# Layer 0's output product: a third pair of row tiles by Strassen's scheme

## The chip, the cores and the metric

The program runs on one core of one Trainium2 chip. The core has five instruction streams. PE is the matrix engine (TensorE), with its weight loads shown apart as PEld. DVE (VectorE) and ACT (ScalarE) do element-wise work, POOL is GpSimd, and SP issues most of the transfers, in the order of its own queue. The metric is the device time of one execution in microseconds (us); lower is better. Three runs of the kernel before lie between 919.55 and 919.75, with a median of 919.62.

## What is computed

Two layers of a mixer on 256 tokens of width 2048, in float32. Of each layer only the last step, the product with `w_out`, is touched:

```python
h = rmsnorm(x, norm_g[l])
proj = h @ w_in[l]                       # 256 x 2048 by 2048 x 7168
...
y = jnp.concatenate([y_a, y_d, y_m], axis=-1) @ w_out[l]   # 256 x 2048 by 2048 x 2048
x = x + y
```

`y_a` are the first 768 columns of `y` (six tiles of 128, from a gated convolution), `y_d` the next 768 (six heads of differential attention), and `y_m` the last 512 (four heads of attention to the memory tokens).

## The kernel before

**Products in three parts.** PE multiplies a 128 x 128 tile of the turned activations by 128 x 512 weights. To keep float32's precision, each operand is split into a rounded part `hi` (a copy on ACT) and the rest `lo` (a subtraction on DVE), and each product is three matmuls: hi·hi, hi·lo, lo·hi. `block` (line 309) walks over the 16 row tiles (128 of the 2048 rows) in chunks of two: `load_w` (L286) issues a 512 KB load into `raw` (four buffers) on SP, splits it on ACT and DVE into `hi` and `lo` (four chunks' worth of buffers), and 2 row tiles x 2 token tiles x 3 = 12 matmuls use it. So the loads may run up to four chunks ahead of the splits, and the splits up to four chunks ahead of the matmuls.

**Side work.** Everything else hangs on a counter of chunks. `run_side` (L231), called after each chunk, raises the counter by one and takes one step of each generator in `tasks` that is due; a generator's `yield n` makes it due n chunks later, and `later(g, n)` starts it n chunks from now. `settle` (L250) is called before a chunk uses a row tile of the activations: if the tile has not been made yet, it calls `run_side(now=True)`, which takes a step of every waiting generator at once, until it is made. Most instructions may be moved by a scheduler that works before the launch; those given to `keep_in_program_order` (`pin`) keep their order among themselves on their engine. On the chip each engine then takes its instructions strictly in the order so fixed.

**The output product of a layer** (from L1213 on). Column blocks 0 and 1 (512 columns each) are done in the plain way and end in `leave`: `finish` adds the accumulators to the residual `xs`, and in layer 0 `x_next` (L801) is put on the list for the next layer. `x_next` for a quarter q of the columns issues `xd<-xs` (residual to memory, 512 KB), two chunks later `xt<-xd` (four transfers back as strips), two later `turn_strips` (L784, a transpose on DVE), and then `split_T` (L257) for the four row tiles 4q to 4q+3 of the next layer's activations `xT`, two per chunk.

Column blocks 2 and 3, the last 1024 columns, are done together. `near` is the pair of accumulators for block 2 and `far` that for block 3. In layer 0 two pairs of row tiles, (6,7) and (8,9), are multiplied by Strassen's scheme in Winograd's form for all 1024 columns at once, by `seven` (L368): 7 products of 3 matmuls where the plain way has 8. `seven` loads the pair's weights as two `wide` tiles of 512 KB each into the buffers named in `homes`, and takes the sums of the token tiles from `sums`, made ahead by `all_sums` (L1203) and `token_sums` (L353). Four of the seven results are shared through the accumulators `x`; `collect` (L1256) adds them to the residual in three steps, and the second of these ends block 2 with `leave(2, near, n=3)`. The pairs stand at the chunk positions in `places` within the list `rest` of the remaining row tiles, 12 in layer 0. `rest` is walked once for `near` (with the pairs between) and once for `far`. In layer 1, the last, three pairs are taken.

**The next layer** opens with the column block 3 of `w_in`, on row tiles 0 to 11 (the first three quarters, six chunks), then block 0 on the same twelve, and only then the last quarter.

Names of buffers touched: `sums` n lies in tag `mkT0` for n = 0 and in `v` for n = 1; the pairs' `wide` tiles lie in `sh` (first) and in `bgx` and `ga` (second). `bgT` holds the turned gate of the convolution, `mqT` the turned queries and later the convolution's input, `mv` the values of the memory tokens. All three have been read for the last time in layer 0 when the convolution of the layer is done; in layer 1 `bgT`, `mqT` and `mv` are filled anew, `mv` by the generator `fetch` (L1026), 32 chunks after the layer's start.

Of the kernel before, what the change touches and what calls it, by code (L numbers as in the profile page):

```python
# [21 lines left out]
DEPTH = 2  # L22
# [8 lines left out]
MH = W_MEM // P  # L31
# [17 lines left out]
def encoder(ctx: ExitStack, tc: tile.TileContext, x, mem, norm_g, w_in, conv_w, conv_b,  # L49
# [4 lines left out]
    def pool(name, bufs, space=None):  # L54
        kw = {"space": space} if space is not None else {}
        return ctx.enter_context(tc.tile_pool(name=name, bufs=bufs, **kw))
# [4 lines left out]
    keep = pool("keep", 1)  # L61
    tmp = pool("tmp", 2)
# [8 lines left out]
    def nm(s):  # L71
        uid[0] += 1
        return f"{s}_{uid[0]}"
# [279 lines left out]
    def token_sums(stat, k, home):  # L353

        f = tmp.tile([P, 2, SEQ], F32, tag="nat", name=nm("f"), bufs=3)
        pin(nc.vector.tensor_tensor(f, stat[:, 0, k:k + 2, :].bitcast(F32), stat[:, 1, k:k + 2, :].bitcast(F32), ALU.add))
        a11, a21, a12, a22 = f[:, 0, 0:P], f[:, 0, P:SEQ], f[:, 1, 0:P], f[:, 1, P:SEQ]
        s = tmp.tile([P, 4, P], F32, tag="nat", name=nm("sums"), bufs=3)
        yield 1
        pin(nc.vector.tensor_tensor(s[:, 0], a21, a22, ALU.add))  # L360
        pin(nc.vector.tensor_tensor(s[:, 2], a11, a21, ALU.subtract))
        pin(nc.vector.tensor_tensor(s[:, 1], s[:, 0], a11, ALU.subtract))
        pin(nc.vector.tensor_tensor(s[:, 3], a12, s[:, 1], ALU.subtract))
        yield 1
        pin(nc.scalar.copy(home[:, 0], s))
        pin(nc.vector.tensor_tensor(home[:, 1], s, home[:, 0].bitcast(F32), ALU.subtract))
# [331 lines left out]
    spare, yTs, gates, summed_heads = {}, {}, {}, set()  # L698
# [251 lines left out]
    mkT, mv, stm, away = [], [], [], []  # L950
# [86 lines left out]
    while s < DEPTH * KT:  # L1037
        l, k = divmod(s, KT)
# [24 lines left out]
    for l in range(DEPTH):  # L1063
# [18 lines left out]
        for b in order:  # L1082
# [4 lines left out]
            if b == 3:  # L1087
                v = keep.tile([P, NT, W_DIFF], F32, tag="v", name=nm("v"))
                ga = keep.tile([P, NT, W_DIFF], F32, tag="ga", name=nm("ga"))
# [20 lines left out]
        mqT = keep.tile([P, MH, SEQ], F32, tag="mqT", name=nm("mqT"))  # L1110
# [22 lines left out]
        bgT = None  # L1133
# [67 lines left out]
        sums = []  # L1201

        def all_sums(l, yT, sums):  # L1203
            for n, tag in enumerate(("mkT0", "v") if l + 1 < DEPTH else ("mkT0", "mkT1", "v")):
                while tag == "v" and (l, MH // 2 - 1) not in summed_heads:
                    yield 1
                sums.append(keep.tile([P, 2, 4, P], F32R, tag=tag, name=nm("sums")))
                yield from token_sums(yT, CG + 2 * n, sums[n])
                yield 1

        tasks.append(later(all_sums(l, yT, sums), 1))
        acc = x_block([(C_X + NB, 256), (C_C + NB, 256)])
        scaled(both_rows(ux, 4, 6), [a[:, 0:256] for a in acc], R2)  # L1213
# [9 lines left out]
        final = l + 1 == DEPTH  # L1223
# [22 lines left out]
            if b == 0:  # L1246
                leave(b, accs[b])

        places = (2, 6, 8) if final else (2, 6)
        paired = [CG + 2 * n for n in range(len(places))]  # L1250
        homes = [((tmp, tag),) * 2 for tag in ("sh", "e", "sh")] if final else [((tmp, "sh"),) * 2, ((keep, "bgx"), (keep, "ga"))]
        rest = [k for k in heads + convs if not CG <= k < CG + 2 * len(places)]
        near, far = accumulators(), accumulators()
        x = [pl.tile([P, NB], F32, tag=tag, name=nm("x")) for pl, tag in ((ps_s, "s"), (ps_s, "s"), (ps_t, "t"), (ps_t, "t"))]
# [71 lines left out]
```

## Time and profile before

| | |
|---|---|
| median of three runs | 919.62 us |
| profiled execution | 919.16 us, of which the span of the instructions is 917.4 us |
| busy in the span: PE, PEld, DVE, ACT, POOL | 911.9, 757.3, 720.1, 515.8, 38.3 us |
| granted PE clock | 1.0 throughout |
| moved by transfers | 215.15 MB, 235 GB/s in the mean |
| layer 0's last 1024 columns on PE | about 464 to 507 us of the span |

The profile lists for each engine the busy time of its instructions, and its queries list groups of instructions, instructions in order of time, waits, and the busy time of every engine in a stretch of time. A matmul's listed duration covers its whole way through the array; the next one starts well before it ends, so the rate of PE is read from starts, not from durations. `acc<-hi,yT` reads: written by the program's tile `acc`, from `hi` and `yT`. Times in timelines count from the start of the span.

### The profile page before, as it was taken

Reading aid. Unit: us, or ns where it says so; the run is one execution under the profiler, and the core shown is the slowest. Engines: PE = TensorE matmul, PEld = TensorE weight load, DVE = VectorE, ACT = ScalarE, POOL = GpSimd, SP = SyncE. Lnnn points to the kernel's source line nnn. Section 1 sums busy time; section 2 is a strip of 40 time slices with the busy share of each in tenths; the row PEclk is TensorE's granted clock in tenths of the full one; section 3 lists DMA queues with packets and bytes.
Section 4 is the critical chain, followed back from the end, with each engine's and each line's share of the span. In section 5 each row is a group of like instructions: output and inputs, shape, how many; then the busy total and the mean of one; then the engine's idle time right before and its main releaser. Section 6 shows DMA issues by size and latency. Waiting matters only on the chain.

```text
span 917.4 us, 12407 instructions
## 1 busy us (share of the span) xinstructions
PE 911.9 (99%) x4161; PEld 757.3 (83%) x4161; DVE 720.1 (78%) x1293; ACT 515.8 (56%) x798; POOL 38.3 (4%) x68
## 2 busy tenths in 40 slices
PE   9999999999999999999999999999999999999998
PEld 6888888888888888888888888888888888888887
DVE  5579978857799697677789857878898787588786
ACT  5667645675555556445556544578555565546352
POOL 2435010000000000000000000000000000000000
PEclk9999999999999999999999999999999999999999
DMA  8899878886679998979777867986889998968842
GB/s 288 289 243 248 287 247 229 244 222 197 188 206 238 247 256 235 263 243 241 264 215 228 275 203 213 268 239 178 236 231 221 266 260 227 268 215 234 275 161 92
DMA packets 244560, 215.15 MB, mean 235 GB/s; under 512 B 131976, under 2 KB 171720, under 8 KB 244496
## 3 DMA queue, kind: packets, MB, share of 16 engines
q1 hardware_dynamic: 239520, 208.71, 79.3%
q0 software_dynamic: 3776, 4.59, 2.1%
q10 hardware_dynamic: 1200, 1.07, 0.3%
q8 instruction: 32, 0.52, 0.2%
q14 instruction: 32, 0.26, 0.1%
HBM read 193.30 MB, written 21.00 MB: 234 GB/s over the span
## 4 chain that ended last, share of the span: by engine, by line
PE 99%; DMA 0%; ACT 0%; SPq 0%; DVE 0%; issue 0%; ACTq 0%
PE acc L305 92%; PE x L351 2%; PE po L519 1%; PE acc L351 1%; PE s L627 1%; PE po L749 1%; PE s L626 1%; PE acc L933 1%; PE pt L763 0%; DMA raw<-in_w_mem_kv_dram 0%; PE s L683 0%; PE s L681 0%; PE s L682 0%; PE rest L305 0%; ACT hi L915 0%; SPq L833 0%
## 5 line engine op out<-in xcount | busy, mean ns | idle before, releaser
L305 PE MATMUL acc<-hi,xT 128*128 128x512 f32 x1792 | 558.4, 390 | 0.0
L294 ACT CAST hi<-raw 128x1024 fp32r<-128x1024 f32 x270 | 283.9, 1053 | 277.3 <-PE acc L305 200.0
L295 DVE TENSOR_TENSOR lo<-raw,hi 128x1024 fp32r<-128x1024 f32 x270 | 329.0, 1222 | 126.7 <-ACT hi L294 124.5
L305 PEld LDWEIGHTS acc<-hi,xT 128*128 128x128 f32 x1792 | 336.3, 188 | 69.0
L305 PE MATMUL acc<-lo,xT 128*128 128x512 f32 x896 | 349.2, 390 | 0.0
L305 PEld LDWEIGHTS acc<-lo,xT 128*128 128x128 f32 x896 | 168.2, 188 | 33.6
L305 PE MATMUL acc<-hi,yT 128*128 128x512 f32 (+1 forms) x432 | 134.1, 388 | 0.0
L305 PEld LDWEIGHTS acc<-hi,yT 128*128 128x128 f32 x432 | 81.0, 188 | 16.7
L305 PE MATMUL acc<-lo,yT 128*128 128x512 f32 x216 | 83.7, 388 | 0.0
L305 PE MATMUL acc<-hi,memT 128*128 128x512 f32 x248 | 78.0, 392 | 0.0
L305 PEld LDWEIGHTS acc<-hi,memT 128*128 128x128 f32 x248 | 46.2, 188 | 9.3
L916 DVE SCALAR_TENSOR_TENSOR lo<-raw,cva,hi 128x1024 fp32r<-128x1024 f32 (+1 forms) x34 | 41.0, 1218 | 15.4 <-ACT hi L915 15.1
L305 PE MATMUL acc<-lo,memT 128*128 128x512 f32 x124 | 48.0, 391 | 0.0
L305 PEld LDWEIGHTS acc<-lo,yT 128*128 128x128 f32 x216 | 40.6, 188 | 8.4
L915 ACT ACTIVATE hi<-raw,cva 128x1024 fp32r<-128x1024 f32 (+1 forms) x34 | 36.5, 1101 | 12.4 <-DMA raw<-in_w_mem_kv_dram 12.2
L305 PEld LDWEIGHTS acc<-lo,memT 128*128 128x128 f32 x124 | 23.3, 188 | 5.5 <-DVE lo L916 0.8
L377 ACT CAST hi<-wide 128x1024 fp32r<-128x1024 f32 x15 | 15.6, 1050 | 16.3 <-DVE wide L380 6.9
L637 ACT ACTIVATE e<-e,mx 128x256 f32<-128x256 f32 x48 | 23.8, 500 | 1.4 <-DVE mx L633 1.3
L780 POOL DMA_DIRECT2D xt<-in_x_dram x32 | 21.5, 678 | 19.7 <-DVE rsy L189 13.6
L377 DVE TENSOR_TENSOR lo<-wide,hi 128x1024 fp32r<-128x1024 f32 x15 | 18.1, 1220 | 3.5 <-ACT hi L377 3.3
L264 ACT ACTIVATE xT<-xf,gx 128x256 fp32r<-128x256 f32 x32 | 14.3, 503 | 5.7 <-DVE xf L786 5.0
L631 DVE SCALAR_TENSOR_TENSOR e<-dist,s 128x512 f32<-128x512 f32 x24 | 15.7, 680 | 2.2 <-PE s L627 1.7
(210 smaller groups left out, 765.8 us busy)
## 6 DMA issues: line engine op xcount, KB each, us to landing
raw<-in_w_in_dram SPq DMA_DIRECT2D x192, 512.0 KB, 4.6
raw<-in_w_out_dram SPq DMA_DIRECT2D x54, 512.0 KB, 4.8
raw<-in_w_in_dram SPq DMA_DIRECT2D x64, 256.0 KB, 4.3
raw<-in_w_mem_kv_dram SPq DMA_DIRECT2D x30, 512.0 KB, 6.4
d<-sh SPq DMA_DIRECT2D x88, 128.0 KB, 4.2
sh<-d SPq DMA_DIRECT2D x72, 128.0 KB, 4.1
wide<-in_w_out_dram SPq DMA_DIRECT2D x10, 512.0 KB, 7.0
xs<-in_x_dram SPq DMA_DIRECT2D x4, 512.0 KB, 6.3
```

The lines of the kernel that those rows point to most:

```text
L264: both = (nc.scalar.activation(hi, src, AF.Copy, scale=gain), nc.vector.scalar_tensor_tensor(lo, src, gain, hi.bitcast(F32), ALU.mult, ALU ...
L294: nc.scalar.copy(hi, raw)
L295: nc.vector.tensor_tensor(lo_, raw, hi.bitcast(F32), ALU.subtract)
L305: i = nc.tensor.matmul(acc, left, right, start=start, stop=stop)
L351: nc.tensor.matmul(acc, left[a], right[b], start=first and i == 0, stop=last and i == 2)
L377: return ((hi, pin(nc.scalar.copy(hi, src))), (lo, pin(nc.vector.tensor_tensor(lo, src, hi.bitcast(F32), ALU.subtract))))
L519: nc.tensor.matmul(po[:, t, :], eT[:, i, t, k, :], v[:, k, h * P:(h + 1) * P], start=k == 0, stop=k == NT - 1)
L631: nc.vector.scalar_tensor_tensor(e[:, c], dist, -slopes[h], s[c], ALU.mult, ALU.add)
L637: nc.scalar.activation(e[:, c, i], e[:, c, i], AF.Exp, bias=mx[:, c, i:i + 1], accum_out=sm[:, c, i:i + 1])
L780: tc.keep_in_program_order(nc.gpsimd.dma_start(st[:, n], src[n * B:(n + 1) * B].rearrange("p (b r) -> b p r", b=NA)))
L915: both = (nc.scalar.activation(hi[:, j], raw[:, j], AF.Copy, scale=g), nc.vector.scalar_tensor_tensor(lo[:, j], raw[:, j], g, hi[:, j].bit ...
L916: nc.vector.scalar_tensor_tensor(lo[:, j], raw[:, j], g, hi[:, j].bitcast(F32), ALU.mult, ALU.subtract))
```

## The change

In layer 0 `places` becomes (2, 6, 8) as in layer 1: a third pair, row tiles (10,11), is taken by `seven`, and `rest` shrinks from 12 row tiles to 10. The third pair's `wide` tiles lie in `bgT` and `mqT`. Three sets of `sums` are made in layer 0: the second moves to `mv`, the third lies in `v`, and both wait until the last memory heads are done (the second did so before). Layer 1 computes what it did.

```diff
         def all_sums(l, yT, sums):
-            for n, tag in enumerate(("mkT0", "v") if l + 1 < DEPTH else ("mkT0", "mkT1", "v")):
-                while tag == "v" and (l, MH // 2 - 1) not in summed_heads:
+            for n, tag in enumerate(("mkT0", "mv" if l + 1 < DEPTH else "mkT1", "v")):
+                while n > 0 and (l, MH // 2 - 1) not in summed_heads:
                     yield 1
...
-        places = (2, 6, 8) if final else (2, 6)
+        places = (2, 6, 8)
         paired = [CG + 2 * n for n in range(len(places))]
-        homes = [((tmp, tag),) * 2 for tag in ("sh", "e", "sh")] if final else [((tmp, "sh"),) * 2, ((keep, "bgx"), (keep, "ga"))]
+        homes = [((tmp, tag),) * 2 for tag in ("sh", "e", "sh")] if final else [((tmp, "sh"),) * 2, ((keep, "bgx"), (keep, "ga")), ((keep, "bgT"), (keep, "mqT"))]
         rest = [k for k in heads + convs if not CG <= k < CG + 2 * len(places)]
```

## The prediction

> **What bounds the kernel now.** I read the busy shares first, then what PE waited for, then the chain that ended last.
>
> ```profile
> PE 911.9 (99%) x4161; PEld 757.3 (83%) x4161; DVE 720.1 (78%) x1293; ACT 515.8 (56%) x798; POOL 38.3 (4%) x68
> PE warm L128 <- DVE zeros L123: 1.2, 1, 1.2
> PE acc L933 <- ACT hi L915: 0.8, 1, 0.8
> 398.90 68.04 PE acc L305 x300
> ```
>
> The second and third lines are all of PE's waits, 2.0 us, both in the start-up. After that PE never stands still, so there is no stall to win back: time can be gained only by fewer matmuls, and is lost as soon as PE waits. The last line, a stretch of the chain, gives PE's pace: 68.04/300 = 0.227 us a matmul.
>
> DVE is 78% busy in the mean, but a mean hides the place where the change lies. The next rows are busy times of two stretches (columns: stretch, then PE, PEld, DVE, ACT, POOL, clock, DMA share, GB/s).
>
> ```profile
> 472.00:504.00 32.00, 32.00 (x142) 26.38 (x141) 31.81 (x39) 19.52 (x28) 0.00 (x0) 1.00 0.68 212
> 506.00:520.00 14.00, 14.00 (x64) 11.58 (x63) 12.83 (x32) 8.01 (x13) 0.00 (x0) 1.00 0.94 315
> ```
>
> From 472 to 504 DVE is busy for 31.81 of 32 us, while PE lives on splits made ahead. ACT has 12.5 us free, and the transfers are at 0.68; behind the layer's end they are at 0.94. So DVE is the second bound here. What it does, in order of time:
>
> ```profile
> 471.75 0.69 DVE L377 TENSOR_TENSOR one<-wide,one 128x512 fp32r<-128x512 f32 x1 [0.34 <-ACT one L377]
> ...
> 478.81 1.22 DVE L295 TENSOR_TENSOR lo<-raw,hi 128x1024 fp32r<-128x1024 f32 x1
> 479.95 2.03 DVE L786 STREAM_TRANSPOSE xf<-xt 128x1024 f32<-128x1024 f32 x1
> 481.92 2.31 DVE L295 TENSOR_TENSOR lo<-raw,hi 128x1024 fp32r<-128x1024 f32 x2
> 484.15 1.66 DVE L265 SCALAR_TENSOR_TENSOR xT<-xf,gx,xT 128x256 fp32r<-128x256 f32 x4
> ...
> 486.87 0.68 DVE L1262 TENSOR_TENSOR xs<-u,xs 128x512 f32<-128x512 f32 x1
> 487.47 1.22 DVE L295 TENSOR_TENSOR lo<-raw,hi 128x1024 fp32r<-128x1024 f32 x1
> ...
> 490.94 1.98 DVE L786 STREAM_TRANSPOSE xf<-xt 128x1024 f32<-128x1024 f32 x1
> ...
> 495.16 0.67 DVE L1230 TENSOR_TENSOR xs<-acc,xs 128x512 f32<-128x512 f32 x1
> ...
> 506.10 2.01 DVE L786 STREAM_TRANSPOSE xf<-xt 128x1024 f32<-128x1024 f32 x1
> ```
>
> 471.75 to 478.81 is the second pair's whole preparation, 7.06 us without a gap. L786 and L265 are the next layer's quarters 0 and 1 being turned. The row at 495.16 ends `finish` of column block 2, at 495.83; the row at 506.10 turns that block's quarter 2.
>
> **The change part by part.**
>
> *Matmuls.* A pair costs 24 in the plain way and 7 x 3 = 21 in `seven`: 3 x 0.227 = 0.68 us less. Nothing hides or adds to that, since PE is full. This is the whole possible gain, 0.07% of the time. The Trainium skill ("TensorE: Matmul & The Clock Gate", Back-to-back issue gap) has a sustained 131 ns for matmuls of 512 columns; by it the gain would be an estimated 0.39 us. The trace here shows 227, which decides.
>
> *Transfers and ACT.* Two `wide` loads of 512 KB replace two `raw` loads of 512 KB. On SP the new pair stands behind these:
>
> ```profile
> 464.17 0.92 SPq L373 DMA_DIRECT2D wide<-in_w_out_dram  x2
> 465.13 0.43 SPq L804 DMA_DIRECT2D xd<-xs  x1
> 474.17 1.81 SPq L770 DMA_DIRECT2D xt<-xd  x4
> ...
> 495.86 0.37 SPq L804 DMA_DIRECT2D xd<-xs  x1
> ...
> 501.26 1.81 SPq L770 DMA_DIRECT2D xt<-xd  x4
> ...
> 509.31 0.37 SPq L804 DMA_DIRECT2D xd<-xs  x1
> ...
> 512.57 2.09 SPq L770 DMA_DIRECT2D xt<-xd  x4
> ```
>
> The new loads fit into the hole between 465.56 and 474.17, in which SP only waits for `xd` to land, and are needed after 480: cost 0. They wait for `bgT` and `mqT`, whose last reader is the convolution:
>
> ```profile
> 443.04 0.42 DVE L1170 TENSOR_TENSOR z<-z,bgT 128x256 f32<-128x256 f32 x1
> 379.63 0.75 DVE L736 TENSOR_TENSOR ga<-mv,v 128x256 fp32r<-128x256 f32 x2
> 410.99 1.22 DVE L295 TENSOR_TENSOR lo<-raw,hi 128x1024 fp32r<-128x1024 f32 x1 [0.70 <-ACT hi L294]
> 402.40 0.69 DVE L356 TENSOR_TENSOR f<-yT 128x512 f32<-128x512 f32 x1
> L360 DVE TENSOR_TENSOR sums<-f x5: 284/285/285, 402.0 to 819.9; 128x128 f32<-128x128 f32 x5
> L366 DVE TENSOR_TENSOR sums<-sums,sums x5: 645/684/686, 405.1 to 822.7; 128x512 fp32r<-128x512 f32 x5
> ```
>
> That is 22 us earlier, so no wait. ACT gets 3 x 1.05 + 0.62 instead of 2 x 1.05, 1.7 us more in 12.5 free. The third set of sums costs DVE 0.69 + 4 x 0.28 + 0.68 = 2.5 us near 405; `mv` has been read by 380.4, and at 410.99 DVE waits for ACT again, thus has caught up: 0. Without that cover it would cost at most its 2.5 us.
>
> *DVE in the crowded stretch.* The new pair adds 7.06 and takes out two splits, one of `near` and one of `far`. L295 costs 1.13 start to start where it stands in a row of work (487.47 to the next instruction), so 4.8 us come in. They come ahead of things that are pinned behind them, and PE has two dates there.
>
> First date: the pair itself. DVE would begin it at 481.92, behind the split at 478.81 and the turn. PE reaches it when the second pair (21 matmuls from 477.25) and one chunk (12) are done, 477.25 + 33 x 0.227 = 484.75, that is 2.8 us after DVE begins. Layer 1 does the same sequence without the turn:
>
> ```profile
> 887.76 0.68 DVE L377 TENSOR_TENSOR one<-wide,one 128x512 fp32r<-128x512 f32 x1
> 892.41 2.50 DVE L377 TENSOR_TENSOR lo<-wide,hi 128x1024 fp32r<-128x1024 f32 x2
> 892.80 0.39 PE L351 MATMUL acc<-hi,yT 128*128 128x512 f32 x1
> 896.50 0.39 PE L351 MATMUL acc<-lo,yT 128*128 128x512 f32 x1
> 477.25 0.62 PE L351 MATMUL x<-one,yT 128*128 128x512 f32 x2
> ```
>
> There PE begins 5.0 us after DVE, and the last `lo` is ready at 894.9, 1.6 us before its first use at 896.50. With 2.2 us less lead the pair is 0.6 late. Bounds: 0 (some of the order can be moved) and 2.0 (the whole turn). I take 0.4; it isn't added below, since what PE loses here it has not to wait for at the second date.
>
> Second date: quarter 2 of the next layer. This is a chain of steps counted in chunks. Let T be the counter at the start of `near`. Before, `near` has 6 chunks and 2 pairs, `far` 6: the second pair is at T+5, `collect` follows five later, and ends block 2 at T+10; `xd` goes out at T+13, `xt` at T+15, the turn at T+17, row tiles 8, 9 at T+18. The layer ends at T+14, and its fifth chunk (which uses row tile 8) comes behind T+18: in time, with none to spare. After, `near` has 5 chunks and 3 pairs, `far` 5. The third pair is at T+7, `collect` starts at T+11 instead of T+9 and ends block 2 at T+12; the layer ends at T+13. Then `xd` at T+15, `xt` at T+17, and the fifth chunk asks for row tile 8 behind T+17: `settle` will force the turn and the split right there, and with them every other waiting step (quarter 3's `xd` and `xt`, and `fetch`, 512 KB meant for 32 chunks later).
>
> In time: before block 2 is finished DVE must do, from 478.81, eight splits of 1.13 (two chunks after the pair 2, five of `far`, one of the next layer), the pair 7.06, two turns of 1.95, eight L265 of 0.40, four L1262 and two L1230 of 0.60: 9.0 + 7.1 + 3.9 + 3.2 + 3.6 = 26.8, so at 505.6. (The same sum for before, 7 splits, no pair, four L265, gives 17.0 and 495.8; the row says 495.83.) With one split fewer or more: 504.5 to 506.8. From there the rows of before take 506.10 - 495.83 = 10.3 us to the turn, 2.0 for it, and then
>
> ```profile
> 508.25 0.91 ACT L264 ACTIVATE xT<-xf,gx 128x256 fp32r<-128x256 f32 x2
> 504.12 0.62 PE L305 MATMUL acc<-hi,xT 128*128 128x512 f32 x2
> 506.62 0.39 PE L305 MATMUL acc<-hi,yT 128*128 128x512 f32 x1
> ```
>
> 0.5 for row tile 8's `hi`: 505.6 + 12.8 = 518.4. PE: the layer's last matmul starts at 506.62; by then two of the next layer's have been pulled ahead (504.12), and row tile 8 comes after 48 of them. That is 506.62 + 47 x 0.227 = 517.3 before, 516.6 after. PE would stand **1.8 us**. From this I take off 0.5: the order of PE is fixed beforehand by readiness, and the row at 504.12 shows two matmuls (0.45) of later work put ahead. I take 1.3. Bounds: 0 below (`xd` to `xt` took 3.3 at 509.31 instead of 5.4; or the next column block's chunks, 12 x 0.227 = 2.7 each, fill the gap), and above 1.8 + 1.2 (late split) + 3.6 (`xd` to `xt` took 9.0 at 465.13) = 6.6.
>
> *Sum.* -0.68 + 1.3 = +0.6. The profiled execution took 919.16 (917.4 of span and 1.8 around it), so 919.8 by its own time; against the median, 919.62 + 0.6 = **920.2**. A measurement of this kernel tells about 0.2% from no change, 1.8 us; this is within.
>
> **The rivals.**
>
> *All of it is hidden*, and only the three matmuls show: 918.9. For it speaks that no wait of PE follows the start-up, though DVE is full for 32 us, so the order made beforehand keeps such dates well; that a chunk or two of another column block would cover 1.8 us; and that `xd` has landed in 3.3. Against it, that quarter 2's turn begins 11 us ahead of its use (506.10 and 517.3) and moves by ten, with 2.5 us of work still behind it. The Trainium skill ("DMA: Bandwidth & Descriptors", Anatomy of one DMA) prices a transfer at 2.0 us and its bytes at 436 GB/s, an estimated 3.2 for 512 KB, so 6.4 for both ways instead of 10.3, which would give this case; the rows at 465.13 and 495.86 are slower than that, the one at 509.31 agrees.
>
> *Slower: the forced steps meet full queues.* The place is SP behind the next layer's fifth chunk. Quarter 2's `xd` and `xt`, quarter 3's and `fetch` are 5 x 512 KB that now fall together into 506 to 520, where the transfers already are at 0.94, and the loads of weights stand behind them on SP. If `xd` to `xt` takes 9.0 again, PE stands 1.8 + 3.6 = 5.4 us: 919.62 - 0.68 + 5.4 = 924.3; with 1.5 us of contention instead of 3.6 it is 922.2; I take 923. It decides from a wait of 2.5 us on (2.5 - 0.68 = 1.8). Against it: loads are issued four chunks ahead and splits another four, and `fetch` waits for nothing.
>
> *The new buffers make the pair wait*, for `mv`, `v`, `bgT` or `mqT`: the pair would come some 5 us later, 924. Their last readers lie 22 us and more ahead, so this is unlikely. That the change doesn't take effect, I rule out: positions and lists depend on nothing else.
>
> **How the numbers follow.** Forecast 0.37 (920.2, own range 919.5 to 921.4), all hidden 0.28 (918.9), full queues 0.30 (923, from 921.5 to 924.5), buffers 0.03; 0.02 for a gain that I can't see. The range reaches from all hidden, 918.8, to 923.8 within the full queues. Within 0.2% lie the forecast and the hidden case: 0.65. Slower by more: 0.33. Faster by over 1.8 us would need more than the three matmuls: 0.02.
>
> **What would show it.** Three matmuls fewer in L305 and L351 together; DVE full from 472 on to about 508; `finish` of block 2 near 505 instead of 495; its turn near 516 instead of 506. Right, if PE has a wait of 1 to 2 us before row tile 8, released by `xT`; hidden, if none; full queues, if it is over 2.5 or the releaser is a load. Wrong in another place, if PE waits at the third pair by more than a microsecond (the first date), or in the next layer for `acc`, whose buffer block 2 leaves only at 505.

## The result: 0.96% slower, and where the time went

The changed kernel takes 927.77 us in the median of five runs (926.51 to 929.74), beside 919.55 of the kernel before in the same series; the ratio is 1.0096, 95% interval [1.0079, 1.0114], or 8.8 us more (by the means, 927.98 and 919.12; the medians lie 8.2 apart). The forecast was 920.2 and the range ended at 923.8.

The profiled execution took 926.91 us, with a span of 924.8 instead of 917.4. From its page, the busy times and the chain that ended last by engine:

```profile
PE 914.3 (99%) x4158; PEld 757.3 (82%) x4158; DVE 726.5 (79%) x1305; ACT 517.2 (56%) x801; POOL 38.2 (4%) x68
PE 91%; DVE 4%; DMA 3%; issue 1%; ACT 1%; SPq 0%; DVEq 0%; ACTq 0%
```

PE's waits, each as its sum, number and longest in us:

```profile
PE acc L351 <- ACT hi L377: 1.7, 2, 0.9
PE acc L305 <- ACT xT L264: 1.4, 1, 1.4
...
PE x L351 <- ACT hi L377: 1.0, 1, 1.0
...
PE acc L305 <- DVE lo L295: 0.6, 1, 0.6
```

The three matmuls are gone (4158 for 4161). The chain, which had been 99% PE, now runs through VectorE, ACT and transfers for most of the other 9%, and PE has four kinds of waits that it did not have. Measured from start to start of its matmuls, as excess over the pace of 0.227 us, PE lost: 1.1 us at the second pair, 2.5 at the third, 0.4 at the split of the chunk behind it, 1.7 before row tile 8 of the next layer, 0.9 at a split right behind that, and 1.6 by a slower clock. That is 8.2 us; less the 0.7 of three matmuls it makes 7.5, beside the 7.4 by which the span grew (917.4 to 924.8). Between 440 and 700 us PE lost nothing else.

SP's transfers of the changed kernel (start, duration of the issue, what):

```profile
455.92 0.94 SPq L373 DMA_DIRECT2D wide<-in_w_out_dram  x2
456.95 0.54 SPq L804 DMA_DIRECT2D xd<-xs  x1
...
466.49 1.81 SPq L770 DMA_DIRECT2D xt<-xd  x4
468.35 0.92 SPq L373 DMA_DIRECT2D wide<-in_w_out_dram  x2
...
509.38 0.37 SPq L804 DMA_DIRECT2D xd<-xs  x1
...
515.17 2.08 SPq L770 DMA_DIRECT2D xt<-xd  x4
...
518.30 0.46 SPq L1028 DMA_DIRECT2D mv<-mvd  x1
```

The loads at 455.92 are the third pair's, by the program's numbering of the tiles; the trace agrees, since the second pair's first copy on ACT (at 473.75) waits 3.81 us for a `wide` load, one of those at 468.35. They stand one microsecond ahead of quarter 0's `xd`, 25 us before anything needs them. `xd` to `xt` then took 9.5 us (456.95 to 466.49) instead of the 5.4 of before (456.92 to 462.31), and the second pair's loads, which stand behind that `xt`, went out at 468.35 instead of 464.17. VectorE shows what came of it:

```profile
474.41 0.69 DVE L377 TENSOR_TENSOR one<-wide,one 128x512 fp32r<-128x512 f32 x1 [3.21 <-ACT one L377]
...
482.60 1.98 DVE L786 STREAM_TRANSPOSE xf<-xt 128x1024 f32<-128x1024 f32 x1
484.51 0.65 DVE L377 TENSOR_TENSOR one<-wide,one 128x512 fp32r<-128x512 f32 x1
...
508.68 0.67 DVE L1230 TENSOR_TENSOR xs<-acc,xs 128x512 f32<-128x512 f32 x1
...
519.95 1.98 DVE L786 STREAM_TRANSPOSE xf<-xt 128x1024 f32<-128x1024 f32 x1 [3.53 <-DMA xt<-xd]
521.86 1.17 DVE L295 TENSOR_TENSOR lo<-raw,hi 128x1024 fp32r<-128x1024 f32 x1
523.03 1.21 DVE L295 TENSOR_TENSOR lo<-raw,hi 128x1024 fp32r<-128x1024 f32 x1
```

The second pair begins at 474.41 instead of 471.75, after an idle stretch of 3.21 us just ahead of the crowded time; the third at 484.51 (481.92 in the prediction); block 2 ends at 509.3 (505.6). Ahead of 519.95 VectorE stands 3.53 us for quarter 2, and two splits stand behind that turn; for one of them PE waits. The last loss is the clock. PE's rows:

```profile
522.52 0.50 PE L305 MATMUL acc<-hi,xT 128*128 128x512 f32 x1 [1.44 <-ACT xT L264]
...
524.29 0.56 PE L305 MATMUL acc<-lo,xT 128*128 128x512 f32 x1 [0.58 <-DVE lo L295]
...
525.08 0.63 PE L305 MATMUL acc<-lo,xT 128*128 128x512 f32 x1
525.50 1.05 PE L305 MATMUL acc<-hi,xT 128*128 128x512 f32 x2
```

The busy times of that stretch (its length, then PE, PE's weight loads, VectorE, ACT and POOL, the granted clock, and the transfers' share and rate):

```profile
524.00:528.20 4.20, 3.91 (x10) 3.09 (x11) 3.99 (x15) 0.60 (x1) 0.00 (x0) 0.59 1.04 324
```

From 525 to 528 the matmuls start 0.43 us apart instead of 0.227. The granted clock (the column behind POOL's) is 0.59 in the mean of the stretch shown, and 0.50 from 525 to 528 alone. The 1.6 us hold for the profiled execution: over the whole program the five runs were granted 0.998, 0.998, 0.998, 0.996 and 1.0, and the one at 1.0 is the longest, 929.74, so the clock is not what makes the kernel slower.

### The profile page after: what moved, and what is told of

Same layout as the page of the kernel before. It is cut to its first block, busy times and chain, and to the rows that moved or that the text cites. A ratio compares the mean times of both kernels' runs of the same rounds, so it can differ in the third digit from the quotient of the medians.

```text
span 924.8 us, 12418 instructions
## 1 busy us (share of the span) xinstructions
PE 914.3 (99%) x4158; PEld 757.3 (82%) x4158; DVE 726.5 (79%) x1305; ACT 517.2 (56%) x801; POOL 38.2 (4%) x68
## 4 chain that ended last, share of the span: by engine, by line
PE 91%; DVE 4%; DMA 3%; issue 1%; ACT 1%; SPq 0%; DVEq 0%; ACTq 0%
PE acc L305 85%; DMA xd<-xs 2%; DVE lo L295 1%; PE po L519 1%; PE x L351 1%; PE acc L351 1%; PE s L627 1%; PE po L749 1%; PE s L626 1%; DVE wide L380 1%; DMA wide<-in_w_out_dram 1%; PE pt L763 0%; DVE xf L786 0%; SPq L770 0%; DVE lo L377 0%
## 5 line engine op out<-in xcount | busy, mean ns | idle before, releaser
L305 PE MATMUL acc<-hi,yT 128*128 128x512 f32 (+1 forms) x416 | 129.5, 388 | 0.0
L305 PEld LDWEIGHTS acc<-hi,yT 128*128 128x128 f32 x416 | 78.0, 188 | 16.1
L305 PE MATMUL acc<-lo,yT 128*128 128x512 f32 x208 | 80.7, 388 | 0.1
L377 ACT CAST hi<-wide 128x1024 fp32r<-128x1024 f32 x18 | 18.7, 1048 | 21.9 <-DVE wide L380 12.3
L377 DVE TENSOR_TENSOR lo<-wide,hi 128x1024 fp32r<-128x1024 f32 x18 | 21.8, 1219 | 3.6 <-ACT hi L377 3.4
L786 DVE STREAM_TRANSPOSE xf<-xt 128x1024 f32<-128x1024 f32 x8 | 16.0, 1997 | 7.0 <-DMA xt<-xd 7.0
```

Of the source, the lines that this page charges most:

```text
L305: i = nc.tensor.matmul(acc, left, right, start=start, stop=stop)
L377: return ((hi, pin(nc.scalar.copy(hi, src))), (lo, pin(nc.vector.tensor_tensor(lo, src, hi.bitcast(F32), ALU.subtract))))
L786: tc.keep_in_program_order(nc.vector.transpose(whole.rearrange("p j (n i) -> p j n i", i=B), st.rearrange("p n (c j) -> p j n c", j=QT)))
```

## The experiments

Each ran beside runs of the kernel before on the same chip; ratios are to those. Experiments 2, 5, 8 and 9 are made from the kernel before, and 2, 8 and 9 do some work besides whose result nothing uses. The others are made from the changed kernel. Line numbers move where an edit adds lines.

**1. The loads held behind xd.** Theory Q: the queue jump is the cause. Rival, theory D: VectorE's added work is.

```diff
+            behind.append(pin(... the xd transfer of x_next ...))
...
-            pin(nc.sync.dma_start(raw..., w[...]))
+            i = pin(nc.sync.dma_start(raw..., w[...]))
+            if behind:
+                tc.add_manual_dep(i.ins, behind[-1].ins.name, ... NoSync ...)
```

> The changed kernel, its third pair's two wide loads held on SP behind the latest xd transfer. Theory Q (queue): those loads, issued 1 us ahead of quarter 0's xd, made xd land 4 us later, hence xt, the second pair's loads and its preparation on VectorE 2.7 us later, and every later date with it. Then the waits at the second pair (1.1 us) and most of those at the third pair (2.5) and at quarter 2 (1.7 + 0.9, and 1.7 of lowered clock behind them) go: 921.5 us or less, near the 920.2 of the prediction. Theory D (VectorE): its 4.8 us of added work on a full engine are the cause, the queue adds only the wait at the second pair: 926 us.

Measured: 924.09 us, ratio 1.0054 [1.0042, 1.0067], 5.0 us over before. SP in this run:

```profile
456.86 0.37 SPq L809 DMA_DIRECT2D xd<-xs  x1
461.66 1.81 SPq L775 DMA_DIRECT2D xt<-xd  x4
463.51 0.92 SPq L373 DMA_DIRECT2D wide<-in_w_out_dram  x2
...
465.34 2.60 SPq L373 DMA_DIRECT2D wide<-in_w_out_dram  x2
...
506.51 0.37 SPq L809 DMA_DIRECT2D xd<-xs  x1
512.79 1.81 SPq L775 DMA_DIRECT2D xt<-xd  x4
```

And PE's waits:

```profile
PE acc L305 <- ACT xT L264: 1.5, 1, 1.5
...
PE acc L305 <- DVE lo L295: 0.6, 1, 0.6
PE acc L351 <- ACT hi L380: 0.4, 1, 0.4
```

The dates up to the third pair are those that the prediction had assumed (461.66, 463.51, new loads at 465.34), the wait at the second pair is gone, that at the third falls from 2.5 to 0.6. Quarter 2's waits and the lowered clock stay. Neither theory had it right alone: the queue jump is 0.42% of the 0.96%, some 3.9 us by the ratios. By what PE lost in the two profiled executions, 8.2 and 5.2 us, it is some 3.

**2. The early loads alone**, in the kernel before, into buffers that nothing reads.

```diff
+        def extra_loads(near):
+            for j, tag in enumerate(("bgT", "mqT")):
+                t = keep.tile([P, 2, NB], F32, tag=tag, name=nm("extra"))
+                pin(nc.sync.dma_start(t..., w_out[l][(10 + j) * P:(11 + j) * P, 2 * NB:4 * NB]))
...
+              between={..., 8: extra_loads}
```

> The kernel before (two pairs), with two more 512 KB loads into the third pair's buffers that nothing reads, issued at the same place of SP's queue as in the changed kernel. Theory Q: xd lands about 4 us later, the second pair is about 2.7 us late on VectorE and PE waits about 1 us there; behind it the lead of the splits (1.7 us at the least) takes the rest: 920.5 us. If the transfers are harmless by themselves: 919.5 us and no wait of PE.

Measured: 920.41 us, ratio 1.0018 [1.0009, 1.0027], 1.7 us. SP's rows:

```profile
455.84 0.94 SPq L1294 DMA_DIRECT2D extra<-in_w_out_dram  x2
456.87 0.38 SPq L804 DMA_DIRECT2D xd<-xs  x1
466.74 1.82 SPq L770 DMA_DIRECT2D xt<-xd  x4
468.60 1.78 SPq L373 DMA_DIRECT2D wide<-in_w_out_dram  x2
```

PE's wait:

```profile
PE acc L351 <- ACT hi L377: 1.2, 1, 1.2
```

With no work added to any engine, two loads at this place hold `xt` back by 4.4 us (466.74 for 462.31), and PE waits at the second pair; start to start it lost 2.4 us there, where about 1 was expected. That shows the mechanism by itself. (These two loads come on top of the others; in the changed kernel they replace two of `raw`.) Whether the jump costs more in the changed kernel is not shown: 3.9 and 1.7 have intervals of some 2 and 1 us, and the profiled executions give some 3 and 2.4.

**3. collect two chunks sooner**, the loads left in front.

```diff
-                    tasks.append(later(collect(near), 5))
+                    tasks.append(later(collect(near), 5 if final else 3))
```

> The changed kernel, with collect begun three chunks behind the third pair instead of five, so that column block 2 ends two chunks sooner; the loads still jump the queue. If quarter 2's date is a cost of its own, its waits (1.7 + 0.9) and the lowered clock behind them (1.7) go: 923.5 us. If VectorE's total is the limit, the work only trades places and the splits come late instead: 926 us or more.

Measured: 925.83 us, ratio 1.0073 [1.0060, 1.0087]. Better than the changed kernel by 0.2%, at the edge of what the intervals tell apart, and nearer to the second theory's 926 than to the first's 923.5. But the edit did little of what it was meant to: block 2 ends only 2 us sooner (`xd` at 507.33). PE still loses 2.6 at the next layer and 4.8 at the pairs and the split behind them (4.0 in the changed kernel), while the clock stays at 1.0.

**4. Both edits**, of the first and the third experiment.

> Both edits: loads behind xd, collect two chunks sooner. If queue and date are all of the loss, 919 us (three matmuls saved, at most 0.4 us of wait at the third pair). If VectorE's added work costs something by itself, PE still waits at the third pair or for a split: 920 to 922 us.

Measured: 921.01 us, ratio 1.0025 [1.0015, 1.0036], 2.3 us over before. `xd` of quarter 2 goes out at 503.17, the clock stays up, and PE loses 0.6 at the third pair, 0.4 at the split behind it, and 1.4 in the next layer. So queue and date are most of the loss, not all.

**5. The forced date alone**: the kernel before, quarter 2 put off.

```diff
-                leave(2, near, n=3)
+                leave(2, near, n=5)
```

> The kernel before (two pairs, no added VectorE work), with quarter 2's xd put off by two chunks (n=5 for 3), so that settle forces its turn and split as in the changed kernel; block 2 itself still ends near 496. If the forced date alone costs what the changed kernel lost there (waits of 2.6 and 1.7 of lowered clock), 922 to 923 us. If the cost is that VectorE ends block 2 ten us later, quarter 2 has its lead here and the time is that of before, within 0.3 us.

Measured: 918.89 us, ratio 1.0002 [0.9993, 1.0011]: no cost, though `settle` forces here too. `xd` is ready early, and SP's rows show that it was sent when it was ready, not when its step fell due:

```profile
494.48 0.37 SPq L804 DMA_DIRECT2D xd<-xs  x1
500.48 1.81 SPq L770 DMA_DIRECT2D xt<-xd  x4
```

On VectorE the turn follows without a wait:

```profile
510.81 2.02 DVE L786 STREAM_TRANSPOSE xf<-xt 128x1024 f32<-128x1024 f32 x1
```

The chain of chunk counts is therefore not what costs. What is left is the time at which VectorE ends block 2; experiment 11 tests that.

**6. No force**: the fourth experiment with collect a further chunk sooner, so that nothing is forced.

```diff
-                    tasks.append(later(collect(near), 5 if final else 3))
+                    tasks.append(later(collect(near), 5 if final else 2))
```

> The changed kernel with its loads behind xd and collect begun two chunks behind the third pair, one sooner than in the fourth experiment: quarter 2's split falls due before the fifth chunk, and nothing is forced (quarter 3's xt and fetch stay at their dates). If the forced steps in the queues are what is left at the next layer (1.2 us), 919.7 us; if it is VectorE's late end of block 2, as the fourth experiment: 921 us.

Measured: 921.32 us, ratio 1.0029 [1.0018, 1.0041]; not told apart from the fourth. Block 2 ends at 505.4 even so: the order made beforehand put splits and turns ahead of its last addition. This run doesn't tell whether the forced steps cost anything: PE's loss in the next layer fell from 1.4 to 0.5, and 1.5 came in at a split at 497.5, which the fourth didn't have. The fifth is what speaks on that.

**7. The turns of quarters 0 and 1 sent out later**, on top of the sixth.

```diff
-                leave(b, accs[b])
+                leave(b, accs[b], n=9)
...
-                      homes[n], (lambda: leave(1, accs[1], pin, 4)) if n == 0 else lambda: None)
+                      homes[n], (lambda: leave(1, accs[1], pin, 6)) if n == 0 else lambda: None)
```

> The sixth experiment, and quarters 0 and 1 sent out later (n=9 for 5, n=6 for 4), so that their turns on VectorE come behind the third pair and behind block 2's end. If the turn at 482.6 and VectorE's total ahead of block 2's end cause the rest, the wait at the third pair (0.6 + 0.4) goes and block 2 ends some 5 us sooner: 918.3 us, 0.6 under before. If VectorE has no room at all, the splits of the next layer come late instead: 920 us or more.

Measured: 926.81 us, ratio 1.0085 [1.0071, 1.0099]. The waits at the pairs are all gone, and one other took everything back. VectorE:

```profile
479.50 0.69 DVE L380 TENSOR_TENSOR one<-wide,one 128x512 fp32r<-128x512 f32 x1
...
505.76 0.70 DVE L1235 TENSOR_TENSOR xs<-acc,xs 128x512 f32<-128x512 f32 x1
...
520.01 1.98 DVE L791 STREAM_TRANSPOSE xf<-xt 128x1024 f32<-128x1024 f32 x1 [5.35 <-DMA xt<-xd]
521.91 1.18 DVE L295 TENSOR_TENSOR lo<-raw,hi 128x1024 fp32r<-128x1024 f32 x1
```

PE's wait:

```profile
PE acc L305 <- DVE lo L295: 6.1, 1, 6.1
```

The third pair begins at 479.50, ahead of the turn, which settles its wait. But block 2 still ends at 506, VectorE stands idle for 5.35 us ahead of quarter 2's turn, and a split that PE needs first is queued behind it. The clock fell too (0.54 in the mean from 523 to 528), which cost some 2 us more. Half of the hypothesis fell: later dates for the turns didn't bring block 2's end forward.

**8. The third set of sums alone**, in the kernel before, not used.

```diff
-            for n, tag in enumerate(("mkT0", "v") if l + 1 < DEPTH else ("mkT0", "mkT1", "v")):
-                while tag == "v" and (l, MH // 2 - 1) not in summed_heads:
+            for n, tag in enumerate(("mkT0", "mv" if l + 1 < DEPTH else "mkT1", "v")):
+                while n > 0 and (l, MH // 2 - 1) not in summed_heads:
```

> The kernel before with a third set of sums made (mkT0, mv, v as in the changed kernel) and not used. By the prediction VectorE has caught up within 6 us and it costs nothing: as before within 0.3 us. If not, up to the 2.5 us of its VectorE work.

Measured: 918.76 us, ratio 0.9999 [0.9990, 1.0008]. The 2.5 us of sums cost nothing.

**9. VectorE's work alone**: four more subtractions of 128x1024 in the kernel before.

```diff
+        def extra_work(near):
+            t = keep.tile([P, 2, NB], F32, tag="bgT", name=nm("extra"))
+            for _ in range(4):
+                pin(nc.vector.tensor_tensor(t, xs[:, :, 0:NB], xs[:, :, 0:NB], ALU.subtract))
...
+              between={..., 8: extra_work}
```

> The kernel before (two pairs) with four more subtractions of 128x1024 on VectorE, 4.8 us, where the third pair would stand, into a buffer that nothing reads. Added work alone moves the end of block 2 from 496 to about 501; quarter 2 then has row tile 8 at 513.5, 3.8 us before PE asks for it. If the loss in the changed kernel needs the later place of collect and of quarters 0 and 1 besides (theory: dates), this costs nothing, within 0.3 us. If 4.8 us on a full VectorE cost by themselves, splits come late: 920.5 us or more.

Measured: 919.62 us, ratio 1.0009 [1.0000, 1.0018]. Between nothing and 1.7 us, nearer to the first: 4.8 us more on a VectorE that is full for 32 cost about a third of themselves at the most. VectorE (the end of block 2, then quarter 2's turn):

```profile
502.23 0.67 DVE L1230 TENSOR_TENSOR xs<-acc,xs 128x512 f32<-128x512 f32 x1
...
513.76 1.99 DVE L786 STREAM_TRANSPOSE xf<-xt 128x1024 f32<-128x1024 f32 x1 [1.13 <-DMA xt<-xd]
```

PE has lost 0.2 us in the profiled execution. So this amount alone is not the limit, but it uses up the lead: row tile 8's `hi` is ready at 517.0 (508.8 before), just when PE asks for it.

**10. Only quarter 0's turn later**, on top of the fourth.

```diff
-                leave(b, accs[b])
+                leave(b, accs[b], n=7)
```

> The fourth experiment (loads behind xd, collect two chunks sooner) with quarter 0 alone sent out two chunks later (n=7 for 5), so that its turn comes behind the third pair, and quarter 1 as it was. The wait at the third pair (0.6 + 0.4) goes as in the seventh experiment; if nothing moves behind the turn of quarter 2 that PE needs first, 920 us, otherwise 921 us or more. Below the time of before only if block 2 also ends sooner than 503.

Measured: 920.81 us, ratio 1.0019 [1.0010, 1.0028]. The wait at the pairs is gone; PE loses 0.5 at 509.5, and 1.4 and 0.9 at quarter 2, whose `xd` goes out at 504.01. The time is nearer to the expected 921 than to 920: what was won at the pairs was lost again in the next layer.

**11. The turns held behind block 2's end**, on top of the seventh: what VectorE does is the same, the order is not. The edit does two things: it pins the additions that end block 2, and it holds the turns behind the last of them.

```diff
-                leave(2, near, n=3)
+                leave(2, near, lambda i: ended.append(pin(i)), n=3)
...
+        if ended:
+            tc.add_manual_dep(i.ins, ended[-1].ins.name, ... NoSync ...)   # i: the transpose in turn_strips
```

> The seventh experiment, with the turns of quarters 0 and 1 held on VectorE behind the last addition that ends block 2. If it is the order of VectorE's work and not its amount that costs the rest, block 2 ends near 497 as before the change, quarter 2 has its lead again, the third pair has no wait, and only the three matmuls show: 918.3 us beside 918.9 of before, 0.6 under it and just at what can be told. If the amount is the limit, quarters 0 and 1 are late for the next layer's first chunks instead: 920 us or more.

Measured: 918.47 us beside 918.85, ratio 0.9998 [0.9989, 1.0008]. VectorE (the end of block 2, then quarter 0's turn):

```profile
496.67 0.68 DVE L1237 TENSOR_TENSOR xs<-acc,xs 128x512 f32<-128x512 f32 x1
...
497.87 2.01 DVE L791 STREAM_TRANSPOSE xf<-xt 128x1024 f32<-128x1024 f32 x1
```

SP:

```profile
452.79 0.94 SPq L373 DMA_DIRECT2D wide<-in_w_out_dram  x2
...
456.24 0.38 SPq L811 DMA_DIRECT2D xd<-xs  x1
...
465.08 1.80 SPq L775 DMA_DIRECT2D xt<-xd  x4
...
497.38 0.44 SPq L811 DMA_DIRECT2D xd<-xs  x1
...
503.95 1.81 SPq L775 DMA_DIRECT2D xt<-xd  x4
```

All of PE's waits:

```profile
PE warm L128 <- DVE zeros L123: 1.2, 1, 1.2
PE acc L940 <- ACT hi L922: 0.2, 1, 0.2
PE acc L305 <- DVE xT L265: 0.2, 1, 0.2
```

Block 2 ends at 497.3, quarter 2 is out at 497.38, and all that PE waits for behind the start-up is 0.2 us (0.5 counted start to start). With three pairs in both layers and the same instructions as in the changed kernel, the whole loss of 8.8 us is gone. Which of the edit's two parts does it was not told apart. The loads are not behind `xd` in this run: quarter 0's `xd` goes out later in the program, so the second pair's loads are held by nothing and go to 452.79, and `xd` to `xt` takes 8.8 us. So a late `xt` did no harm here, where no pair's loads stand behind it and the turn comes at 497.87. The remaining gain of three matmuls, 0.7 us, can't be told from none: the interval holds 1.

## Why the prediction was wrong, step by step

**Right:** what bounds the kernel (PE without slack, VectorE full from 472 on), the 0.68 us of three matmuls (4158 for 4161), the sums at no cost (8), buffers that are free in time, and the two places where PE would wait.

**The step that failed is "Transfers and ACT", where the new loads were given the hole on SP between 465.56 and 474.17 and a cost of 0.** That took the order of the program for the order of the queue. The front of this document says that pinned instructions keep their order among themselves; the trace shows that they don't: in the program these loads come behind quarter 0's and quarter 1's `xd`, and on SP they stand ahead of both (455.92, 456.95, 469.31). An instruction is pinned only behind the one that the program makes just before it on its engine, which for the third pair's loads was the `raw` load of a chunk, itself not pinned and drawn far ahead (issued by 455.87). With their buffers free since 443 the loads followed it at 455.92, ahead of `xd`. Whoever reads that a buffer is free 22 us ahead should have asked what the load will collide with when it comes early. I asked only whether it would be late. Experiments 1 and 2 show the price: 3.9 us in the changed kernel, 1.7 by itself, where the sum had 0. The prediction's own sign of being wrong in another place, over a microsecond at the third pair, is what came: 2.5.

**The first date** (the third pair) was set at 0.4 us. With the queue in order it is 0.6, and 0.4 more at the next split (1); the turn of quarter 0 ahead of the pair is its cause (7, 10 and 11 move it, and the wait is gone).

**The second date** (quarter 2) had the right mechanism and too small a size. In experiment 1, where the queue is as the prediction assumed, block 2 ends at 506.5 (505.6 was worked out), and PE loses 1.80 us before row tile 8 where 1.3 was forecast. Both sides of that difference had moved: row tile 8 was there at 519.7 instead of 518.4, with 0.9 of it from block 2's end and 0.4 from the way there and back; PE, which had lost 1.0 at the first date, got to it at 517.6 instead of 516.6. That is 2.1 us, less the 0.45 of two matmuls that were pulled ahead, as the 0.5 in the prediction had it (50 of the next layer's matmuls start before the wait, 48 were counted). So the size came out as close as it did in part by luck. Behind it came a split queued behind the waiting turn, 0.84, which stood in the bounds (1.2) but not in the forecast, and half the clock for some 3 us, 1.52, which stood nowhere. Together 4.2 instead of 1.3. The bound of 6.6 held.

**The rivals.** "Full queues" (923, up to 924.5) and "buffers" (924) were the nearest in time, and both wrong in their mechanism. The forced steps did follow, but behind quarter 2's own transfers (`xd` and `mv` at 517.84 and 518.30, `xt` at 515.17), and those were hardly slower for it: from block 2's end to the turn it took 10.6 us (509.35 to 519.95) where the rows of before took 10.3, and `xd` to `xt` 5.8, not 9.0. The same forcing in experiment 5 costs nothing. The transfers that mattered were those at 456, not at 506 to 520. And the new buffers were not late but free too early. In "all hidden", 6.4 us had been estimated for both ways; they took most of these 10.6.

**What the sum missed as a whole:** it counted VectorE's work and took its order from the program. Experiment 9 shows that the amount alone just fits, and 11 that the order decides: the same work costs 8.8 us in the changed kernel, 2.3 in the fourth experiment and nothing in the eleventh. Why the order made beforehand puts block 2's last addition behind splits and turns that could wait was not looked into.

## What to carry to other kernels

A load whose buffer is free early is not harmless on a queue that is served in order: it can go ahead of transfers that others wait for (here 1.7 us alone), so look at what will stand behind it, and tie it to the place where it is wanted. Where an engine is full but its total fits, work out which of its instructions releases the longest chain, and put that one first; between experiments 7 and 11, which differ only in pinning those additions and holding the turns behind them, that order is worth 0.9%, while the whole gain of the change is 0.07%. Ahead of a saving that small, list the dates that the change moves on every queue.

## What the runs showed of the hardware

The granted clock fell after waits of PE that were short: to half in the changed kernel, from 524.6 to 528.0, after losses of 1.7 and 0.9 us within 4 us, and likewise in experiment 1 (1.8 and 0.8, then half from 521.9 to 525.3); each time it cost 1.5 to 1.6 us more. It did not fall behind the third pair of the changed kernel, where PE lost 2.5 us within 4, nor in 3 at the same place, nor in the profiled execution of 10 after 1.4 and 0.9. So the sum of what is lost nearby does not decide.

Each of these two half-speed stretches is 3.41 us long. In every one of these runs the time from the clock's rise in the start-up to its fall is a whole number of such stretches (151 in the changed kernel, 150 in 1). Counted off from that rise, they sort all these cases. The changed kernel lost 2.3 us of the one just before the fall (521.18 to 524.59, PE busy for 1.49), experiment 1 2.2 (518.52 to 521.93, busy for 1.62). At the third pair the changed kernel lost 2.0 in one (487.05 to 490.46, busy for 1.72) and experiment 3 1.95 (487.72 to 491.13, busy for 1.74), and the clock stayed. In 10 the two losses fall into two stretches, 1.0 and 1.2. The edge of these runs lies thus between 2.0 and 2.2 us lost in one stretch; it rests on four stretches. In 7, where PE waited 6.1 us, half the clock lasted for two of them.

The Trainium skill ("TensorE: Matmul & The Clock Gate", What's actually happening) has the clock halved after an idle window of about 3.4 us that runs freely. The length and the free running agree with these stretches. But in the changed kernel and in 1 no wait was so long, and PE was at work between the two, so by these two runs less than a whole idle window can be enough.
